# Splitting two feature groups of the last MLP by pairs of tiles

## Chip, cores, metric

The kernel runs on one core of one Trainium2 chip, alone. The metric is the device time of one execution in microseconds (us); the number given for a kernel is the median of its runs.

## What is computed

One transformer block for 1024 tokens of width 1024: a mixer of two sparse attentions, cross-attention to a memory of 256 tokens, and an MLP, each added to the residual stream.

```
x = x + mixer(rms_norm(x, norm1_g), ...)
x = x + memory_xattn(rms_norm(x, norm2_g), mem, ...)        # 4 heads of 128, w_xq, w_xk, w_xv, w_xo
x = x + square(relu(rms_norm(x, norm3_g) @ w_ff_in)) @ w_ff_out   # 1024 -> 4096 -> 1024
```

All values are float32. Where precision asks for it, the kernel splits an operand into a high part in a short format (hi, `xh`, `whi`, `hh`) and the remainder (lo, `xl`, `wlo`, `hl`), and multiplies hi by hi, hi by lo and lo by hi, so that one product is three matmuls.

## The kernel before

The 1024 tokens are eight tiles of 128. After the projections, the work runs in two streams that are written side by side: the sparse attention of tile after tile, and beside it whatever is ready of the rest. The rest goes through `between` (L902: output projection of the mixer, then memory attention) and `mlp` (L1002). `between` takes two tiles at a time, `mlp` four. When the sparse attention is through, what remains is `between` of tiles 4 and 5 (in pool `dn`) beside `between` of tiles 6 and 7 (in pool `d2`), and then `mlp` of tiles 4 to 7, alone.

The instruction order on each engine is not the program's: the tile framework schedules it from a timeline of its own (`schedule_with_timeline_sim`), and each engine, and SP's queue of DMA issues, then goes through its list in order.

In `mlp`, 4096 features are eight groups (`f4`) of 512. For each group the first layer makes four PSUM tiles of 128 features by all tokens of the call (512 columns, stationary `w_ff_in`, moving `xh`, `xl`; 24 matmuls each). ScalarE takes the relu and the square (L1034, L1035), GpSimd the split into `hh` and `hl` (L1037, L1038, ring `h` of eight buffers). The second layer then makes, for each half `c` of the output columns and each tile, one PSUM tile (12 matmuls, stationary `hh`, `hl`, moving `w_ff_out`), which VectorE adds to the residual stream `x2` (L899). TensorE writes these PSUM tiles in turn to two buffers.

Weights come by `load_w` (L251): a DMA into ring `wraw`, the cast `whi` on ScalarE (L244) and the remainder `wlo` on GpSimd or VectorE (L249, two of three on GpSimd in this last part, `PLAN_TAIL`). A group needs sixteen such loads of 256 KB. Rings of pool `d2` for it: `wraw` 3, `whi` 6, `wlo` 6. `between` loads its own weights whole, without a split, into the rings `whi` and `wlo` by turns (`load_whole`, L261).

Before the MLP stands a norm (`norm_T2`, L290): a square with a sum on ScalarE (L293), a power on GpSimd, and for each half of a tile a product with the gain on VectorE (L297), four transposes on TensorE into PSUM (L274), then hi on ScalarE and lo on VectorE (L235, L236). The gain (`gain2`, L340) lies in two buffers of ring `h`.

At the end of memory attention, for two heads at a time (`memory_item`, L939): scores, exponentials (L966), transposes of the probabilities (L972), values, and a store of the result to memory (L986), which is read back (L992), transposed and multiplied by `w_xo`. After `between` of tiles 4 and 5 the residual stream goes out to memory (L1000) and is read back by `mlp` (L1007); that of tiles 6 and 7 stays in its buffers.

Of the kernel before, what the change touches and what calls it, by code (L numbers as in the profile page):

```python
# [22 lines left out]
P = 128  # L23
# [13 lines left out]
    "p1": {"x4": 5, "st": 2, "relu": 4, "wraw": 4, "whi": 6, "wlo": 6, "c8": 4, "c4": 2, "kraw": 5, "pc": 2},  # L37
    "p2": {"x4": 3, "st": 1, "relu": 2, "whi": 4, "wlo": 4, "c8": 3, "c4": 1, "kraw": 4, "pc": 2},
    "dn": {"b4": 4, "h": 8, "relu": 2, "wraw": 2, "whi": 4, "wlo": 4},
    "d2": {"b4": 4, "h": 8, "relu": 2, "wraw": 3, "whi": 6, "wlo": 6},  # L40
}
PSUMS = {"p1": {"D": 4, "M": 3, "C": 1}, "main": {"S": 2, "PT": 2, "PV": 1, "D": 2, "M": 1}}
TAGS = {"p1": ("D", "M", "C"), "p2": ("D", "M", "D"), "dn": ("D", "M"), "d2": ("S", "PT")}
PLAN_HEAD = ("ag", "av")
PLAN_MAIN = ("ag",)
PLAN_TAIL = ("ag", "av", "ag")
# [37 lines left out]
def drain(gen):  # L84
    for _ in gen:
        pass
# [19 lines left out]
def merge(a, b):  # L106
    drain(beside(*a, *b))
# [59 lines left out]
def build(nc, tc, I, C, out):  # L167
# [13 lines left out]
    def pst(tag, shape):  # L181
        return psum["pool"].tile(shape, F32, tag=tag, name="ps" + tag, bufs=psum["n"][tag],
                                 padded_shape=[P, 512 // int(np.prod(shape[2:]))] + list(shape[2:]))

    def ring(pool, tag, shape, dt=F32):
        n = RINGS[pool.name if isinstance(pool.name, str) else "dn"][tag]
        return pool.tile(shape, dt, tag=tag, name=tag, bufs=n)
# [63 lines left out]
    def load_w(pool, shape, *srcs):  # L251
        raw = ring(pool, "wraw", shape)
        for dst, src in srcs:
            nc.sync.dma_start(dst(raw), src)
        hi, lo = ring(pool, "whi", shape, F32R), ring(pool, "wlo", shape, F32R)
        split_w(raw, hi, lo)
        return hi, lo
# [32 lines left out]
    def norm_T2(pool, x_t, gb, xs):  # L290

        ss = small(pool, "nss", 1)
        s.activation(xs[0], x_t.rearrange("p (k c) -> p k c", c=P), AF.Square, accum_out=ss)  # L293
        r = rsqrt_of(pool, ss, DM, 1, "n")
        for c in range(0, DM, 512):
            xn = ring(pool, "relu", [P, 512])
            v.scalar_tensor_tensor(xn, x_t[:, c:c + 512], r[:, 0:1], gb[c // 512], op0=ALU.mult, op1=ALU.mult)  # L297
            to_T(pool, xn, [x[:, c // P:c // P + 4] for x in xs], 4)
# [29 lines left out]
    def xT(pool, nt, whole=False):  # L328

        parts = [pool.tile([P, DM // P, nt * P], F32 if whole else F32R, tag="x" + n, name="x" + n)  # L330
                 for n in ("h" if whole else "hl")]
        return (parts, [lambda t, k, x=x: x[:, k, t * P:(t + 1) * P] for x in parts],
                lambda t: [x[:, :, t * P:(t + 1) * P] for x in parts])
# [668 lines left out]
    def mlp(pool, t0, nt, x2s):  # L1002
# [13 lines left out]
        for f4 in range(8):  # L1016
# [24 lines left out]
            for c in range(2):  # L1041
# [4 lines left out]
                for t in range(nt):  # L1046
# [11 lines left out]
                                          x2[t][:, c * 512:(c + 1) * 512])  # L1058
                    yield 2.6

    def pe_stack():
        pe = p1.tile([P, 2, 32], F32R, tag="pe", name="pe")
        pe2 = ring(p1, "relu", [P, 2, 2, 64])
        for j in range(2):
            nc.sync.dma_start(pe2[0:32, :, j, :], W["nsa_cmp_pe"].rearrange("k l d -> l k d"))
        pp = pst("M", [P, 2, 32])
        for kv in range(2):
            te.transpose(pp[:, kv, :], pe2[0:32, kv, :, :].rearrange("p a d -> p (a d)"), ident[0:32, 0:32])
        s.activation(pe, pp, AF.Copy)
        v.tensor_tensor(pe[64:128], pp[64:128], pe[64:128], op=ALU.subtract)  # L1070
        return pe
# [49 lines left out]
    d2_pool = tc.tile_pool(name="d2", bufs=1, side="right", reuse_waits="tile")  # L1121
    plan["w"] = PLAN_TAIL
    d2 = d2_pool.__enter__()
    x2s = {}
    rest = (w for w in rest if not isinstance(w, tuple))
    merge((rest, REST), (between(d2, 6, 2, x2s, True), 45.0))
    dn_pool.__exit__(None, None, None)
    drain(mlp(d2, 4, 4, x2s))
    d2_pool.__exit__(None, None, None)
    ctx.close()  # L1130

# [20 lines left out]
```

## Time and profile before

| | |
|---|---|
| median of 3 runs | 1833.72 us (1833.55 to 1837.51) |
| profiled execution | 1835.75 us, its span 1833.9 us |
| mean clock granted to TensorE | 0.97 |
| busy share PE, PEld, DVE, ACT, POOL | 94%, 80%, 51%, 59%, 49% |

PE is TensorE's matmuls and PEld its weight loads, DVE is VectorE, ACT ScalarE, POOL GpSimd, SP the engine that issues most DMAs. In a timeline a row is start, length, engine, line, instruction, output and inputs by the program's names without buffer numbers, shape, count, and in brackets the idle time before it and what ended that. Matmuls overlap, so the distance of two starts, not the length, is what one costs. In a row of windows, the length is followed by the busy time (and number of instructions) of each engine, the clock granted to TensorE (1.00 is full), the share of DMA engines in use and the GB/s moved.

### The profile page before, as it was taken

The page shows a single profiled execution, that of the slowest core. Times are in us where ns is not written, and L with a number is a line of the kernel's source. Part 1 is how long each engine was busy: PE and PEld are TensorE (multiplying, and loading weights), DVE is VectorE, ACT ScalarE, POOL GpSimd, SP SyncE. Part 2 cuts the span into 40 slices and gives each one's busy share as a digit, 9 for nine tenths or more (in the row PEclk, how much of TensorE's full clock was granted, in tenths as well). Part 3 has the DMA queues.
Part 4 walks back from the last instruction along what each step waited for, and adds up shares of the span by engine and source line. Part 5 has one row for each costly group of instructions (what it writes and reads, how often), then busy time and mean ns, then how long its engine had stood idle before and what let it go on. Part 6 is the DMA issues. An engine that isn't in the chain of part 4 may idle for free. (4 is left out here: it accounts for less than half of the span.)

```text
span 1833.9 us, 28049 instructions
## 1 busy us (share of the span) xinstructions
PE 1726.9 (94%) x9262; PEld 1474.2 (80%) x9262; DVE 936.1 (51%) x2353; ACT 1074.6 (59%) x2687; POOL 895.0 (49%) x1034
## 2 busy tenths in 40 slices
PE   5996999889989998999999999999999799999999
PEld 5995988777878787778887788888988578787787
DVE  4553766575684678466664656646523422222222
ACT  4444658889588669955797457994412323333332
POOL 2364657446262244677676576662111144454443
PEclk9997998999999999999999999999989799999999
DMA  8224512256335320222112112125394222222232
GB/s 203 70 87 160 103 34 79 78 193 180 122 112 162 120 81 24 73 81 71 64 63 91 54 65 75 60 79 185 99 288 131 71 69 92 92 93 93 94 99 98
DMA packets 180081, 187.50 MB, mean 102 GB/s; under 512 B 34656, under 2 KB 149088, under 8 KB 179936
## 3 DMA queue, kind: packets, MB, share of 16 engines
q1 hardware_dynamic: 172000, 175.23, 30.8%
q0 software_dynamic: 7936, 10.49, 2.2%
q8 instruction: 73, 1.20, 0.3%
q14 instruction: 72, 0.59, 0.1%
HBM read 164.69 MB, written 20.97 MB: 101 GB/s over the span
## 5 line engine op out<-in xcount | busy, mean ns | idle before, releaser
L249 POOL TENSOR_TENSOR wlo<-wraw,whi 128x512 fp32r<-128x512 f32 (+1 forms) x230 | 308.5, 1347 | 278.7 <-ACT whi L244 247.6
L244 ACT ACTIVATE whi<-wraw 128x512 fp32r<-128x512 f32 (+2 forms) x289 | 181.1, 628 | 247.4 <-PE psS L218 147.1
L218 PE MATMUL psD<-whi,xh 128*128 128x256 f32 (+1 forms) x704 | 193.8, 359 | 3.6 <-ACT whi L244 2.9
L218 PE MATMUL psD<-wlo,xh 128*128 128x256 f32 (+1 forms) x704 | 194.8, 357 | 0.8 <-DMA wlo<-in_w_in_dram 0.8
L236 DVE TENSOR_TENSOR pl<-psPT,ph 128x512 fp32r<-128x512 f32 (+1 forms) x232 | 142.2, 621 | 78.2 <-ACT ph L235 75.4
L218 PE MATMUL psD<-whi,h 128*128 128x512 f32 x512 | 174.3, 404 | 1.8 <-POOL h L1037 1.0
L688 ACT ACTIVATE S<-S,mn 128x128 f32<-128x128 f32 (+7 forms) x192 | 142.7, 744 | 41.5 <-DVE mn L686 40.3
L218 PE MATMUL psS<-whi,h 128*128 128x512 f32 x512 | 162.1, 392 | 5.1 <-DVE b L899 5.1
L693 POOL TENSOR_SCALAR S<-S,sums,gi 128x640 f32<-128x640 f32 (+7 forms) x128 | 107.7, 850 | 106.7 <-DVE sums L691 99.0
L235 ACT ACTIVATE ph<-psPT 128x512 fp32r<-128x512 f32 (+1 forms) x232 | 122.8, 540 | 60.9 <-PE psPT L703 54.5
L249 DVE TENSOR_TENSOR wlo<-wraw,whi 128x512 fp32r<-128x512 f32 (+1 forms) x59 | 64.3, 1090 | 166.9 <-ACT whi L244 166.8
L218 PEld LDWEIGHTS psD<-whi,xh 128*128 128x128 f32 x704 | 134.0, 198 | 14.3 <-ACT whi L244 3.3
L218 PEld LDWEIGHTS psD<-wlo,xh 128*128 128x128 f32 x704 | 134.8, 197 | 12.5 <-DMA wlo<-in_w_in_dram 1.2
L703 PE MATMUL psPT<-c_ident,S 128*128 128x128 f32 x816 | 132.3, 279 | 8.3 <-DVE ql L236 4.2
L899 DVE TENSOR_TENSOR b<-psS,b 128x512 f32<-128x512 f32 (+1 forms) x80 | 50.0, 635 | 152.6 <-PE psS L218 152.6
L218 PEld LDWEIGHTS psS<-whi,h 128*128 128x128 f32 x512 | 96.1, 188 | 29.3 <-DVE b L899 9.3
L218 PE MATMUL psS<-K,qh 128*128 128x384 f32 (+3 forms) x288 | 113.5, 397 | 5.6 <-DVE mn L686 2.8
L218 PEld LDWEIGHTS psD<-whi,h 128*128 128x128 f32 x512 | 95.6, 190 | 23.7 <-DVE b L899 1.5
L703 PEld LDWEIGHTS psPT<-c_ident,S 128*128 128x128 f32 x816 | 98.1, 143 | 18.9 <-POOL S L693 5.6
L218 PE MATMUL psD<-wlo,h 128*128 128x512 f32 x256 | 102.5, 404 | 1.3 <-POOL wlo L249 1.3
L218 PE MATMUL psD<-xh,wlo 128*128 128x512 f32 x256 | 101.5, 398 | 0.0
L899 DVE TENSOR_TENSOR b<-psD,b 128x512 f32<-128x512 f32 (+1 forms) x112 | 63.2, 572 | 74.5 <-PE psD L218 73.0
(299 smaller groups left out, 4647.4 us busy)
## 6 DMA issues: line engine op xcount, KB each, us to landing
wraw<-in_w_ff_in_dram SPq DMA_DIRECT2D x128, 256.0 KB, 2.7
wraw<-in_w_ff_out_dram SPq DMA_DIRECT2D x128, 256.0 KB, 2.6
whi<-in_w_out_dram SPq DMA_DIRECT2D x32, 256.0 KB, 5.0
wlo<-in_w_out_dram SPq DMA_DIRECT2D x32, 256.0 KB, 4.6
wraw<-in_w_in_dram SPq DMA_DIRECT2D x24, 256.0 KB, 3.1
q<-st SPq DMA_DIRECT2D x12, 512.0 KB, 2.6
qin<-q SPq DMA_DIRECT2D x44, 128.0 KB, 2.3
x<-in_x_dram SPq DMA_DIRECT2D x8, 512.0 KB, 5.2
```

The lines of the kernel that those rows point to most:

```text
L218: te.matmul(o, a, b, start=start, stop=stop)
L235: s.activation(hi, src, AF.Copy)
L236: v.tensor_tensor(lo, src, hi, op=ALU.subtract)
L244: s.activation(hi, raw, AF.Copy)
L249: (v if l == "v" else g).tensor_tensor(lo, raw, hi, op=ALU.subtract)
L688: s.activation(S, S, AF.Exp, bias=low, scale=-1.0, accum_out=sums[:, hh:hh + 1])
L693: g.tensor_scalar(Ss[hh], Ss[hh], sums[:, hh:hh + 1], 1.0 if gate is None else gate[:, hh:hh + 1], op0=ALU.mult, op1=ALU.mult)
L703: te.transpose(p2[:, j, hh, :], S[:, (c + j) * P:(c + j + 1) * P], ident)
L899: v.tensor_tensor(dst, pt, dst, op=ALU.add)
```

## The change

`mlp` for tiles 4 to 7 gives way to a new function, `mlp_tail`, in a pool `d3` of its own with larger rings for split weights (`wraw` 4, `whi` 8, `wlo` 8). Of the eight feature groups the first two are done by pairs of tiles: for tiles 4 and 5 first, then groups 2 to 7 for all four tiles, then groups 0 and 1 for tiles 6 and 7. So these two groups' weights are loaded and split twice, and their first-layer matmuls stream 256 columns. The norm of tiles 4 and 5 comes ahead of the pair's groups, that of tiles 6 and 7 after them in the program. The pool lies where `dn` lay, beside `d2`, in which memory attention of tiles 6 and 7 still runs; `d2` loses `wraw`, and its rings for whole weights go from 6 and 6 buffers to 5 and 5. The PSUM tags are `D` and `M`, before `S` and `PT`; `M` has one buffer, `PT` two. `between` of tiles 6 and 7 no longer keeps the residual stream on chip: it goes out to memory and is read back. The outputs of tiles 4 and 5 leave as one write each when groups 2 to 7 are done.

In the order that the scheduler gives the changed program, the first pair group stands among the last instructions of memory attention of tiles 6 and 7, the second one behind them, and the transposes of the norm of tiles 6 and 7 behind that.

```diff
-    "d2": {"b4": 4, "h": 8, "relu": 2, "wraw": 3, "whi": 6, "wlo": 6},
+    "d2": {"b4": 4, "h": 8, "relu": 2, "whi": 5, "wlo": 5},
+    "d3": {"b4": 4, "h": 8, "relu": 2, "wraw": 4, "whi": 8, "wlo": 8},
...
-TAGS = {"p1": ("D", "M", "C"), "p2": ("D", "M", "D"), "dn": ("D", "M"), "d2": ("S", "PT")}
+TAGS = {"p1": ("D", "M", "C"), "p2": ("D", "M", "D"), "dn": ("D", "M"), "d2": ("S", "PT"), "d3": ("D", "M")}
...
+    def mlp_tail(pool, t0, G):
+
+        x2 = {}
+        (xh, xl), _, xt_of = xT(pool, 4)
+
+        def start(t, gb3):
+            x2[t] = ring(pool, "b4", [P, DM])
+            nc.sync.dma_start(x2[t], x2_dr[t0 + t])
+            norm_T2(pool, x2[t], gb3, xt_of(t))
+
+        def group(f4, ts, last):
+            cols = slice(ts[0] * P, (ts[-1] + 1) * P)
+            n = len(ts) * P
+            hs = []
+            for f2 in range(2):
+                gr = []
+                for k0 in range(0, 8, KG):
+                    c0 = (f4 * 4 + f2 * 2) * P
+                    hi, lo = load_w(pool, [P, KG, 256], (lambda r: r, W["w_ff_in"][k0 * P:(k0 + KG) * P, c0:c0 + 256]
+                                                         .rearrange("(k p) n -> p k n", p=P)))
+                    gr += [(hi[:, k, :], lo[:, k, :]) for k in range(KG)]
+                for f in range(2):
+                    pt = pst(TAGS[pool.name][0], [P, n])
+                    fs = slice(f * P, (f + 1) * P)
+                    for k in range(8):
+                        wh, wl = gr[k]
+                        mm(pt, wh[:, fs], xh[:, k, cols], k == 0, False)
+                        mm(pt, wl[:, fs], xh[:, k, cols], False, False)
+                        mm(pt, wh[:, fs], xl[:, k, cols], False, k == 7)
+                    r = ring(pool, "relu", [P, n])
+                    s.activation(r, pt, AF.Relu)
+                    s.activation(r, r, AF.Square)
+                    hh, hl = ring(pool, "h", [P, n], F32R), ring(pool, "h", [P, n], F32R)
+                    g.tensor_scalar(hh, r, 1.0, 1.0, op0=ALU.mult, op1=ALU.mult)
+                    g.tensor_tensor(hl, r, hh, op=ALU.subtract)
+                    hs.append((hh, hl))
+            for c in range(2):
+                gr = []
+                for k in range(4):
+                    r0 = (f4 * 4 + k) * P
+                    gr.append(load_w(pool, [P, 512], (lambda r: r, W["w_ff_out"][r0:r0 + P, c * 512:(c + 1) * 512])))
+                for t in ts:
...
+                    dst = x2[t][:, c * 512:(c + 1) * 512]
+                    v.tensor_tensor(dst, pt, dst, op=ALU.add)
+                    if last:
+                        nc.sync.dma_start(out[0, (t0 + t) * P:(t0 + t + 1) * P, c * 512:(c + 1) * 512], dst)
+
+        for ts in ((0, 1), (2, 3)):
+            gb3 = gain2(pool, W["norm3_g"])
+            for t in ts:
+                start(t, gb3)
+            if ts[0] == 0:
+                for f4 in range(G):
+                    group(f4, ts, False)
+        for f4 in range(G, 8):
+            group(f4, (0, 1, 2, 3), False)
+        for t in (0, 1):
+            nc.sync.dma_start(out[0, (t0 + t) * P:(t0 + t + 1) * P, :], x2[t])
+        for f4 in range(G):
+            group(f4, (2, 3), f4 == G - 1)
...
-    x2s = {}
     rest = (w for w in rest if not isinstance(w, tuple))
-    merge((rest, REST), (between(d2, 6, 2, x2s, True), 45.0))
+    merge((rest, REST), (between(d2, 6, 2, {}, False), 45.0))
     dn_pool.__exit__(None, None, None)
-    drain(mlp(d2, 4, 4, x2s))
+    with tc.tile_pool(name="d3", bufs=1, reuse_waits="tile") as d3:
+        mlp_tail(d3, 4, 2)
```

More of the change, by code (lines that the diff above doesn't have):

```diff
@@ L1059, in mlp @@
                     yield 2.6
+    def mlp_tail(pool, t0, G):
[37 more added lines that the diff above has]
+                for t in ts:
+                    pt = pst(TAGS[pool.name][0], [P, 512])
+                    us = slice((t - ts[0]) * P, (t - ts[0] + 1) * P)
+                    for f in range(4):
+                        hh, hl = hs[f]
+                        wh, wl = gr[f]
+                        mm(pt, hh[:, us], wh, f == 0, False)
+                        mm(pt, hh[:, us], wl, False, False)
+                        mm(pt, hl[:, us], wh, False, f == 3)
+                    dst = x2[t][:, c * 512:(c + 1) * 512]
[15 more added lines that the diff above has]
+            group(f4, (2, 3), f4 == G - 1)
```

## The prediction

> **What bounds the kernel now.** I read the page first, then the chain of waits, then the windows of the last 400 us, and last the timelines of single engines there.
>
> ```profile
> span 1833.9 us, 28049 instructions
> PE 1726.9 (94%) x9262; PEld 1474.2 (80%) x9262; DVE 936.1 (51%) x2353; ACT 1074.6 (59%) x2687; POOL 895.0 (49%) x1034
> ```
> ```profile
> 1469.14 28.00 PE psS L218 x119
> ...
> 1633.26 44.15 PE psS L218 x191
> ...
> 1677.43 0.70 DVE b L899
> ...
> 1813.53 16.63 PE psS L218 x72
> ...
> 1830.18 0.69 DVE b L899
> ```
>
> The second fence is the chain (start, length, what). From 1469 to 1830 us it is the matmuls of the last MLP and almost nothing else: a feature group is 192 matmuls of 512 columns, 44.15 us and one residual add of 0.70 on which TensorE waits (its PSUM buffer), 44.9 in all. After the last matmul come 3.7 us (1833.9 less 1830.2). So the MLP itself leaves nothing to gain; what can be gained lies just before it:
>
> ```profile
> 1425.00:1430.00 5.00, 4.32 (x18) 3.50 (x19) 1.80 (x5) 2.67 (x8) 0.00 (x0) 0.57 0.30 105
> 1430.00:1435.00 5.00, 3.24 (x16) 3.05 (x15) 0.85 (x2) 0.00 (x0) 0.00 (x0) 0.50 0.21 43
> 1435.00:1440.00 5.00, 3.06 (x9) 2.34 (x10) 0.00 (x0) 0.60 (x1) 0.00 (x0) 0.50 0.33 117
> 1455.00:1460.00 5.00, 1.99 (x12) 1.11 (x10) 2.18 (x7) 4.38 (x9) 2.48 (x4) 0.98 0.28 95
> 1460.00:1465.00 5.00, 3.09 (x13) 2.15 (x12) 4.99 (x9) 2.67 (x5) 0.95 (x2) 0.50 0.00 0
> ```
> ```profile
> 1420.52 0.38 PE L274 MATMUL psPT<-c_ident,relu 128*128 128x128 f32 x2
> 1428.29 4.96 PE L218 MATMUL psS<-h 128*128 128x128 f32 x22 [0.42 <-ACT h L235]
> 1436.25 1.09 PE L274 MATMUL psPT<-c_ident,relu 128*128 128x128 f32 x4 [3.01 <-DMA relu<-xo]
> 1453.81 1.03 PE L218 MATMUL psS<-whi,xh 128*128 128x256 f32 x4
> 1454.68 1.03 PE L218 MATMUL psS<-wlo,xh 128*128 128x256 f32 x4
> 1458.68 1.34 PE L274 MATMUL psPT<-c_ident,relu 128*128 128x128 f32 x8 [2.98 <-DVE relu L297]
> 1468.79 0.78 PE L218 MATMUL psS<-xh,whi 128*128 128x512 f32 x1
> ```
>
> Windows (length, busy PE, PEld, DVE, ACT, POOL, then clock, DMA, GB/s) and TensorE's timeline show one stretch, 1420.5 to 1468.8, 48.3 us: the end of memory attention of tiles 6 and 7, to 1455.5, then 13.3 us in which only the norm of four tiles runs. TensorE has gaps there and is granted half its clock for most of it. All attention work of it, at full clock, is some 22 us (its output projection alone is eight blocks of 1.73: the two rows at 1453.81 and 1454.68, 0.87 apart, are half a block).
>
> **The change: what stays equal.** The MLP keeps its multiplications, but in two feature groups each first-layer matmul now streams 256 columns and is issued twice as often.
>
> ```profile
> 44.31 0.28 PE L218 MATMUL psD<-whi,xl 128*128 128x256 f32 x1
> 44.43 0.29 PE L218 MATMUL psD<-whi,xh 128*128 128x256 f32 x1
> ...
> 1471.29 0.39 PE L218 MATMUL psS<-xh,whi 128*128 128x512 f32 x1
> 1471.52 0.40 PE L218 MATMUL psS<-xh,wlo 128*128 128x512 f32 x1
> ```
>
> At full clock 256 columns start 0.115 to 0.12 us apart and 512 columns 0.23. A pair's group is 96 x 0.115 + 48 x 0.23 = 22.1 us, half of 44.2. TensorE is not charged for the split. The price must come from waits.
>
> **First pair group, beside attention of tiles 6 and 7.** Up to that attention's second half the engines' orders differ little. Then three queues change.
>
> ```profile
> 1411.76 0.34 SPq L1000 DMA_DIRECT2D x<-b  x1
> 1414.48 0.32 SPq L1007 DMA_DIRECT2D b<-x  x1
> 1415.13 0.32 SPq L1000 DMA_DIRECT2D x<-b  x1
> 1419.84 0.32 SPq L1007 DMA_DIRECT2D b<-x  x1
> 1433.74 0.42 SPq L986 DMA_DIRECT2D xo<-relu  x1
> 1436.57 0.32 SPq L992 DMA_DIRECT2D relu<-xo  x1
> ```
> ```profile
> wraw<-in_w_ff_in_dram SPq DMA_DIRECT2D x5, 256.0 KB, 2.7
> b<-x SPq DMA_DIRECT2D x2, 512.0 KB, 3.8
> h<-in_norm_g_dram SPq DMA_DIRECT2D x2, 256.0 KB, 3.4
> ```
>
> The rings of attention's own weights shrink from twelve buffers to ten. I cost that at nothing, since ten are still two column blocks of four ahead; if that cover fails, it is one landing, 2.7 us.
>
> SP: in the changed order the second half of the norm gain goes out before both reloads of x2, and it waits for the store of tile 5 (its buffer lies on that tile's). That store needed from 1415.1 to 1419.8. So tile 4 is reloaded at about 1420.1 (before 1414.5) and lands about 1423; the first MLP weight, behind it, lands about 1424.
>
> ```profile
> 1424.29 0.56 ACT L966 ACTIVATE relu<-psS,xnb,xsc 128x256 f32<-128x256 f32 x1 [1.38 <-DVE xnb L963]
> 1444.52 0.63 ACT L244 ACTIVATE whi<-wraw 128x512 fp32r<-128x512 f32 x1 [1.22 <-PE psS L218]
> 1455.79 1.06 ACT L293 ACTIVATE xh<-b 128x1024 fp32r<-128x1024 f32 x1 [0.28 <-PE psS L218]
> 1460.60 0.68 DVE L236 TENSOR_TENSOR xl<-psPT,xh 128x512 fp32r<-128x512 f32 x1
> 1461.20 0.74 DVE L297 SCALAR_TENSOR_TENSOR relu<-b,nr,h 128x512 f32<-128x512 f32 x1
> ```
>
> ScalarE: ahead of the softmax's first exponentials (1424.3 before) now stand two squares of the norm (1.06 each), five weight casts (0.63) and two copies of the norm. The fifth cast is what costs: four raw buffers, so its load goes out only when VectorE is through with the first weight. Square of tile 5 ends about 1426, first cast 1426.7, its remainder (0.68) about 1428.1, load 2.7, cast to 1431.5, copy, and the exponentials start at about 1432 and 1434 (a sixth cast between them). That is 8 us late. Behind them wait both transposes of the probabilities, the value matmuls and the store.
>
> The Trainium skill, "TensorE: Matmul & The Clock Gate", section "Architectural detail", says that ScalarE and VectorE are strict FIFOs and only TensorE pulls weight loads ahead. By it the 8 us stand; were the queue free to pass a waiting cast, this part would end some 5 us sooner, near 1833 for the whole. No run here shows a pass, and the sum goes by the order of the queue.
>
> TensorE then has 19 pair matmuls at half clock (0.23) ahead of the last ten value matmuls, 4 us more: these end about 1445, before about 1433. The store and reload of the result need 2.8 us from issue to issue (1433.74 to 1436.57) and 2.7 to land: 1450.5. From there I count work without gaps: attention's projection (eight blocks of 1.73, 13.8), the pair's second layer (48 x 0.23 = 11.1) and the last 24 first-layer matmuls (2.8), 27.7 in all, and 2 more for transposes and for the matmuls ahead of the reload. The first pair group and attention end at about 1480, where before the full MLP had begun at 1468.8: 22 us of work taken in for 11.
>
> **Second pair group.** It stands alone, after attention, and its weights arrive as they are split.
>
> ```profile
> 1633.30:1678.20 44.90, 44.35 (x193) 35.91 (x193) 11.39 (x14) 14.79 (x24) 22.23 (x19) 1.00 0.30 94
> 1633.30:1678.20 44.90, 25.08 (x64) 12.03 (x64) 6.06 (x5) 14.77 (x11) 1.00 0.30 94
> 1633.30:1678.20 44.90, 22.26 (x97) 17.86 (x97) 0.00 (x0) 0.00 (x0) 7.64 (x8) 1.00 0.30 94
> ```
>
> These are one full group, its wlo instructions alone and its h alone. GpSimd's 14.77 us for eleven weight remainders stays per group whether two tiles use it or four; its 7.64 for h halves. So 18.6 us must fit into 22.1, and with them the sixteen casts of 0.63 that a pair's group repeats (10.1 on ScalarE, and half as much again for the squares) and sixteen more loads; over two groups 32 each, all beside TensorE unless a queue holds them. It fits, but not in order: a group's last h stands behind two or three remainders of 1.34. On TensorE I count 0.7 for the residual add that holds PSUM and 1.0 for that h, 23.8 a group, and 1 more here because two reloads of x2 stand between the weights: 24.9, to 1505.
>
> **Norm of tiles 6 and 7.** The pair group that should hide it cannot: the gain is loaded into h buffers of the group just running, last read 9 matmuls (2.1 us) before its end, and then takes 3.4 to land and 0.74 for the first product. Its four half-tiles go through one PSUM buffer: a copy (as long as a cast, 0.63) and a remainder (0.68) must follow each set of transposes (1.09) before the next may start, 2.4 us, and one product of 0.74 that VectorE puts between raises the mean to 2.65. Three rounds come before the wide matmuls: -2.1 + 3.4 + 0.74 + 3 x 2.65 = 10, and about 2 for half clock after it: 12, to 1517. Before it was 13.3.
>
> **Sum, on the profiled execution.** 1517 + 6 full groups x 44.9 + 2 pair groups (tiles 6 and 7) x 23.8 + 3.7 = 1837.7, against a span of 1833.9: 3.8 slower. The execution's own time is 1835.75, its overhead 1.9; the median of the runs is 1833.72. I put the difference on the median: 1837.5.
>
> The outputs of tiles 4 and 5 now leave before the last two groups, as two writes on SP's queue that wait for residual adds; behind them stand the second layer's weights of the next group. They are costed at nothing, because the first layer's eight weights, 11 us of TensorE's work, are already past them; if not, the price is a landing of 2.7.
>
> Bounds: end of the first part 1475 (TensorE's own work, 44, after 1420.5, with some 10 us in which nothing is loaded yet) to 1484; second group 22.8 to 27; norm 10 to 14; last groups 22.8 to 26 each. All low: 1826; all high: 1850. I took values near the queue walk, not the middle.
>
> **Rivals.** *Faster (0.21):* the place is the exponentials behind the fifth cast. If store and loads land a microsecond or two sooner each and TensorE has sustained work by 1431, exponentials come 5.5 us sooner and half-clock work shrinks by 3: 1837.5 - 8.5 = 1829. It decides where the exponentials start before 1427. For it: DMA is only 0.3 busy at 1425; against it: no clock row rises before TensorE has worked some 7 us (half clock 1430 to 1440 with 3 of 5 us busy). The same page of the Trainium skill, section "What's actually happening", gives about 3.4 us of sustained work for the rise; by that the time would be nearer to this rival.
> *Slower, starved pairs (0.24):* each group's sixteen weights need one per 1.39 us; a raw buffer's turn is 2.7 + 0.63 + 1.34 = 4.7 for four, 1.17. If a load takes over 3.6 us, or casts wait in line for as long, the turn passes 4 x 1.39 = 5.6 and decides: three lone groups that lose 4 each make 1837.5 + 12 = 1850. For it: other loads took 3.4 and 3.8; against it: DMA at 0.30 in the full group.
> *Forecast (0.55):* the three parts nearly cancel, 1831 to 1844.
>
> **How the numbers follow.** 0.2% is 3.7 us, about what a measurement of this kernel can tell from no change. Faster: the first rival and 0.01 of the forecast, 0.22. Within: 0.25, from the forecast. Slower: the rest of it, 0.29, and the starved pairs, 0.53. Range 1828 to 1850: the rivals' values with both tails left out.
>
> **What would show it.** Right: exponentials of tiles 6 and 7's second heads near 1432; attention's last projection matmul near 1477; wide matmuls only from 1515 on; a gap of 8 to 12 us before them, ended by a gain's DMA. Wrong: no such gap, pair groups over 26 us, full groups other than 44.9, or a changed time before 1400.

## The result and the profile after

The changed kernel takes 1851.26 us (median of 1846.43, 1851.02, 1851.51 and 1852.38) against 1835.28 us before (the three runs above and a fourth, 1836.84): a ratio of 1.0081, 95% interval 1.0059 to 1.0104. It is slower by 15 to 16 us. Run again later beside new runs of the kernel before it took 1850.81 against 1837.87, ratio 1.0072 (1.0053 to 1.0091). The forecast was 1837.5 and the range ended at 1850: the side was right, the size was not.

The profiled execution of the changed kernel is its quickest, 1846.43 us with a span of 1844.3; the rerun's profiled execution took 1851.29 with a span of 1849.2. Both are used below, as "the first profile" and "the rerun". The page of the first profile:

```profile
span 1844.3 us, 28688 instructions
PE 1727.9 (94%) x9454; PEld 1482.4 (80%) x9454; DVE 947.9 (51%) x2364; ACT 1094.0 (59%) x2735; POOL 931.9 (51%) x1071
```

TensorE is busy for 1.0 us more than before, in a span 10.4 us longer. So the price is idle time, as the prediction had it; halving the columns of 96 matmuls a group costs next to nothing (0.3 us a group, below). The chain of waits shows where it lies:

```profile
1471.41 1.74 PE psS L219 x8
...
1477.92 3.52 DMA b<-x
...
1484.60 3.42 POOL wlo L250 x2
...
1504.02 3.85 DMA h<-in_norm_g_dram
...
1516.04 2.07 PE psD L219 x4
...
1591.44 44.43 PE psD L219 x191
1635.87 0.02 issue
1635.90 0.70 DVE b L1113
...
1796.78 1.75 POOL wlo L250
...
1802.41 2.96 DMA wraw<-in_w_ff_in_dram
...
1806.16 1.02 POOL wlo L250
```

Before, nothing but matmuls and a residual add a group (two in some) stood here from 1469 on. Now the chain leaves TensorE in three places: in the second pair group (GpSimd's remainders, behind the reload of x2), at the norm of tiles 6 and 7 (the gain's DMA), and in the first of the two last pair groups (a remainder, then a weight that has not landed, then a remainder again). The same in windows (length, then busy PE, PEld, DVE, ACT, POOL, then clock, DMA share, GB/s): second pair group, wait for the norm, a full group, the two last groups:

```profile
1476.20:1505.80 29.60, 25.67 (x145) 20.97 (x143) 8.27 (x12) 15.55 (x30) 20.54 (x22) 0.94 0.52 170
1505.80:1516.00 10.20, 3.20 (x13) 1.92 (x12) 5.89 (x8) 2.51 (x5) 2.02 (x2) 0.64 0.42 140
1591.40:1636.60 45.20, 44.65 (x192) 36.08 (x192) 11.61 (x14) 14.59 (x24) 22.58 (x19) 1.00 0.28 94
1789.10:1816.10 27.00, 24.29 (x144) 20.85 (x144) 8.53 (x9) 12.03 (x25) 18.19 (x19) 0.94 0.48 156
1816.10:1840.10 24.00, 23.44 (x147) 20.29 (x145) 7.10 (x8) 9.04 (x18) 15.06 (x16) 1.00 0.34 121
```

GpSimd has 20.5 us of work in the second pair group, for which TensorE needs 22.1; the prediction had counted 18.6. Of the two last groups only the first is slow: counted from first matmul to first matmul it takes 27.4 us (28.9 in the rerun) and the last one 23.6 (23.9), near the 23.8 of the forecast. Behind the last one no other group's weights have to be loaded and split. TensorE's timeline says what it waited for there and in the norm:

```profile
1494.89 0.50 PE L219 MATMUL psD<-whi,h 128*128 128x512 f32 x1 [0.87 <-POOL h L1095]
1497.28 0.73 PE L219 MATMUL psD<-whi,h 128*128 128x512 f32 x2 [1.19 <-POOL h L1096]
1508.42 0.89 PE L275 MATMUL psM<-c_ident,relu 128*128 128x128 f32 x4 [2.50 <-DVE relu L298]
1511.64 1.09 PE L275 MATMUL psM<-c_ident,relu 128*128 128x128 f32 x4 [2.32 <-DVE xl L237]
1514.27 1.09 PE L275 MATMUL psM<-c_ident,relu 128*128 128x128 f32 x4 [1.54 <-DVE xl L237]
```

The first two rows wait for the hidden values' split on GpSimd, the last two for the one PSUM buffer to be read out.

SP's queue has waits of its own in the second pair group (in all, times, longest, in us):

```profile
SPq L255 <- POOL wlo L250: 8.1, 8, 2.4
SPq L1069 <- DMA x<-b: 3.9, 1, 3.9
```

In the first row the load of a weight waits for a remainder on GpSimd; until that is made, its raw buffer is not free. In the second the reload of tile 7 waits for its store to land, and the second layer's weights stand behind it.

The part by part account, in span time (first matmul of a part to first matmul of the next; the gap before the wide matmuls counts from the last matmul's end):

| part | forecast | first profile | rerun |
|---|---|---|---|
| end of attention and first pair group | 1480 | 1476.2 | 1479.0 |
| second pair group | 24.9 | 29.6 | 28.5 |
| to the first wide matmul | 10 | 10.2 | 10.3 |
| six full groups, with the slow clock at their start | 2 + 269.4 | 273.1 | 274.5 |
| two last pair groups | 47.6 | 51.0 | 52.8 |
| to the end | 3.7 | 4.2 | 4.2 |
| span | 1837.7 | 1844.3 | 1849.2 |

### The profile page after: what moved, and what is told of

Same layout as the page of the kernel before. It is cut to its first block, busy times and chain, and to the rows that moved or that the text cites. A ratio compares the mean times of both kernels' runs of the same rounds, so it can differ in the third digit from the quotient of the medians.

```text
span 1844.3 us, 28688 instructions
## 1 busy us (share of the span) xinstructions
PE 1727.9 (94%) x9454; PEld 1482.4 (80%) x9454; DVE 947.9 (51%) x2364; ACT 1094.0 (59%) x2735; POOL 931.9 (51%) x1071
## 4 chain that ended last, share of the span: by engine, by line
PE 70%; DVE 9%; ACT 6%; DMA 6%; POOL 5%; issue 4%; SPq 1%; POOLq 0%; DVEq 0%; ACTq 0%
PE psD L219 48%; PE psS L219 9%; PE psPV L219 5%; PE psPT L704 4%; ACT dmask L645 2%; POOL wlo L250 2%; PE psM L275 1%; DMA wraw<-in_w_ff_in_dram 1%; DVE S L687 1%; DVE pl L237 1%; PE psPT L591 1%; DMA wraw<-in_w_ff_out_dram 1%; ACT tkt L647 1%; ACT tks L646 1%; DVE relu L298 1%
## 5 line engine op out<-in xcount | busy, mean ns | idle before, releaser
L219 PE MATMUL psD<-whi,h 128*128 128x512 f32 x1024 | 344.0, 405 | 11.6 <-DVE b L1113 5.0
L245 ACT ACTIVATE whi<-wraw 128x512 fp32r<-128x512 f32 x321 | 200.8, 628 | 227.7 <-PE psD L219 145.3
L219 PEld LDWEIGHTS psD<-whi,h 128*128 128x128 f32 x1024 | 193.3, 190 | 62.7 <-DVE b L1113 8.9
L219 PE MATMUL psD<-xh,wlo 128*128 128x512 f32 (+1 forms) x576 | 212.9, 370 | 0.0
L219 PE MATMUL psD<-xh,whi 128*128 128x512 f32 (+1 forms) x576 | 211.2, 371 | 1.3 <-ACT xh L236 0.7
L219 PE MATMUL psD<-xl,whi 128*128 128x512 f32 (+1 forms) x576 | 212.3, 370 | 0.0
L219 PE MATMUL psD<-wlo,h 128*128 128x512 f32 x512 | 205.3, 403 | 1.3 <-POOL wlo L250 1.3
L219 PEld LDWEIGHTS psD<-xh,whi 128*128 128x128 f32 x576 | 108.5, 189 | 19.4 <-ACT xh L236 1.1
L219 PEld LDWEIGHTS psD<-xh,wlo 128*128 128x128 f32 x576 | 108.7, 189 | 17.5 <-POOL wlo L250 0.3
L219 PEld LDWEIGHTS psD<-xl,whi 128*128 128x128 f32 x576 | 108.6, 189 | 16.0
```

The costliest lines, as they stand in the source:

```text
L219: te.matmul(o, a, b, start=start, stop=stop)
L245: s.activation(hi, raw, AF.Copy)
```

## The experiments

Each kernel was timed beside the kernel before on the same chip; a ratio is against that. "Changed kernel" is the one of the diff. Four theories were put up: A, the turn of the raw weight buffers starves the pair groups that stand alone (the prediction's rival); B, the loss is the uncovered norm; C, the rebuilding costs and not the pairs; D, GpSimd's order of work starves the lone groups.

**again**: no edit.

> The changed kernel once more, unchanged. Its profiled execution had a span of 1844.3 us, its other runs 1848.9 to 1850.3. If the 5 us come from one place (a queue that falls into another order in some executions), a second profile of about 1849 shows where: both theories below put it into the two-tile groups that stand alone (1476 to 1506 and 1789 to 1840 in the first profile). If the profile is again near 1844 and the runs near 1850, the place stays open.

1850.81 us. The second profile is one of the usual length, and no single place holds its 5 us: the reload of x2 is issued 1.2 us later than in the first (1415.75 against 1414.53), the first pair group ends 2.8 later, the norm is 1.7 behind, the two last groups take 1.8 more. So the executions differ by a microsecond or two here and there, and the kernel before varies as much (1832.83 to 1843.74 in that session).

**one_pair_group** and **no_pair_group**: `mlp_tail(d3, 4, 2)` becomes `mlp_tail(d3, 4, 1)`, and `mlp_tail(d3, 4, 0)`. Without pair groups the four writes of tiles 6 and 7's output, which stand in the last one, fall away too.

> Only feature group 0 is done by pairs of tiles; seven groups take all four tiles. Theory A (the two-tile groups that stand alone are starved of split weights): the second pair group, 29.6 us instead of half a full group's 22.6, and the second of the two last ones go, the norm of tiles 6 and 7 follows the first pair group, still uncovered (its residual stream is reloaded at 1476.7 and 1481.5): wide matmuls from about 1489, 2.6 us of half clock, 7 x 45.1, one pair group of 25, 4: a span of 1834 to 1838, 6 to 10 us less than the changed kernel. Theory B (the loss is the uncovered norm and the lone groups cost only their matmuls): the uncovered norm stays, so 1841 to 1845. Theory C (the restructuring, not the pairs, costs): no difference to the changed kernel.

> No feature group is done by pairs; new pool, larger rings, residual stream of tiles 6 and 7 out and back, one PSUM buffer for the norm's transposes all stay. Theory A: attention ends near 1455 as before the change, the store and reload of tiles 6 and 7 (4 + 4 us) and their norm follow: wide matmuls from 1470 to 1476, then 8 x 45.15 and 4: 1835 to 1841. Theory C: as slow as the changed kernel, 1844 or more.

One group: 1841.96 us, ratio 1.0022 (1.0008 to 1.0035); its profile's span of 1840.3 lies 2 us above theory A's range and just below B's. None: 1850.56, ratio 1.0069 (1.0051 to 1.0087), which is some 10 us above what theory A had and as slow as with two. So the loss is not simply "the pairs": without them, the rebuilding alone costs 12 to 13 us. Its chain of waits:

```profile
1442.10 3.44 DMA relu<-xo
...
1452.70 14.13 PE psS L219 x56
...
1467.31 2.81 DMA x<-b
...
1470.13 4.22 DMA b<-x
...
1482.39 2.07 PE psD L219 x4
```

Attention's result comes back from memory at 1445.5, its projection runs to 1466.8 where it ended about 1455.5 before, and then tiles 6 and 7 go out to memory and back (7 us) and through their norm (8 us) with nothing beside them: wide matmuls from 1482.4, before from 1468.8. The first pair group earns most of this back (8.6 us from none to one) by filling attention's gaps; the second, placed alone, gave away what the first had earned (8.9 us from one to two).

**own_gain**: the gain of the last norm loaded once, into two buffers of its own.

```diff
+        gb3 = gain2(pool, W["norm3_g"], "gb")
         for ts in ((0, 1), (2, 3)):
-            gb3 = gain2(pool, W["norm3_g"])
```

> The gain of the last norm is loaded once into two buffers of its own, instead of twice into buffers of the ring of split hidden values; two pair groups stay. The order then has the norm's transposes of tiles 6 and 7 among the second pair group's second layer. Theory A and B: the gap of 10 us before the wide matmuls goes, all but about 2 (the transposes still share one PSUM buffer): 1834 to 1837 against 1844.3. If the gain is not what the norm waits for (the reload of the residual stream or the PSUM buffer is): 1841 to 1844.

1839.96 us, ratio 1.0011 (0.9996 to 1.0025): 11 to 13 us off the changed kernel. Second pair group and norm together take 35.2 us (1476.2 to 1511.4) instead of 39.8, so the gain's wait was worth 4.6 (3.6 against the rerun's 38.8) and not the whole gap; the transposes still wait for each other and for VectorE inside the group. The rest was not expected: from there to the last groups 269.5 us instead of 273.1. Each full group took 44.66 us instead of 45.20, though nothing in it was edited (hidden_ring_last, below). The two last groups took 53.3 us, no less than in the changed kernel.

**more_raw** and **h_on_vector**: larger rings; the hidden values' split of pair groups on VectorE.

```diff
-    "d3": {"b4": 4, "h": 8, "relu": 2, "wraw": 4, "whi": 8, "wlo": 8},
+    "d3": {"b4": 4, "h": 8, "relu": 2, "wraw": 8, "whi": 10, "wlo": 10},
```

```diff
-                    g.tensor_scalar(hh, r, 1.0, 1.0, op0=ALU.mult, op1=ALU.mult)
-                    g.tensor_tensor(hl, r, hh, op=ALU.subtract)
+                    (g.tensor_scalar(hh, r, 1.0, 1.0, ...) if n == 512 else v.tensor_copy(hh, r))
+                    (g if n == 512 else v).tensor_tensor(hl, r, hh, op=ALU.subtract)
```

> Rings of the last MLP only: raw weight buffers 8 instead of 4, split weights 10 and 10 instead of 8 and 8. Theory A (a raw buffer's turn starves the lone pair groups): the second pair group falls from 29.6 us to 24 to 25 and the last two from 51 to 46 to 47, 8 to 10 us off: a ratio to the kernel before of about 1.002 against 1.008. Theory D (GpSimd, which goes in order through remainders and hidden-value splits, starves them): 0 to 3 us off, ratio 1.006 to 1.008.

> In the pair groups VectorE makes both halves of the hidden values' split, GpSimd only the weight remainders; rings as in the changed kernel. Theory D: the second pair group falls to 24 to 25.5 us and the last two to 47 to 48, 6 to 8 us off, ratio 1.003 to 1.005. Theory A: the casts still wait for loads, 0 to 3 us off, ratio 1.006 to 1.008.

more_raw: 1845.89 us, ratio 1.006 (1.0043 to 1.0078). h_on_vector: 1843.05, ratio 1.0035 (1.002 to 1.0049). By the times D explains more than A. Windows of the second pair group and of the two last, first more_raw, then h_on_vector:

```profile
1478.70:1505.70 27.00, 24.10 (x145) 19.68 (x143) 9.32 (x12) 14.31 (x29) 21.21 (x22) 1.00 0.59 189
1789.30:1837.70 48.40, 46.12 (x289) 40.16 (x287) 15.10 (x17) 20.05 (x40) 32.20 (x33) 1.00 0.36 114
```
```profile
1480.00:1507.30 27.30, 23.80 (x145) 19.87 (x143) 14.41 (x20) 15.27 (x30) 14.67 (x14) 1.00 0.59 186
1791.60:1838.90 47.30, 45.51 (x289) 40.31 (x287) 23.63 (x33) 21.10 (x42) 23.68 (x18) 1.00 0.47 150
```

Either edit takes 3 to 5 us out of the last two groups (51.0 and 52.8 without), nearly all of it from the first of them, and 1 to 3 out of the second pair group, so theory D alone is not the whole of it either. They are not exclusive: a late weight and a full GpSimd hold TensorE by turns, as the chain of the changed kernel had it (remainder, DMA, remainder). more_raw also made the rings of split weights larger, so it does not show by itself that it was the raw ring; SP's waits for remainders, above, speak for that.

**keep_67**: the residual stream of tiles 6 and 7 stays on chip, as before the change (`between(d2, 6, 2, x2s, True)`, and `start` takes the kept buffer).

> The changed kernel, but the residual stream of tiles 6 and 7 stays in its buffers, as before the change: no store, no reload, and the second pair group's weights no longer stand behind that reload on SP. If these two reloads hold that group (the prediction gave them 1 us): its 28.2 to 29.6 us fall by 2 to 4, ratio 1.005 to 1.0065. If GpSimd's order alone does: under 1 us, ratio 1.007 to 1.008. The norm of tiles 6 and 7 still waits for the gain, so its gap stays near 10 us.

1848.99 us, ratio 1.0056 (1.0036 to 1.0077); 3 to 5 us off by the ratios, whose intervals overlap. The window is clearer: with the store and the reload gone from SP's queue the second pair group takes 25.4 us, 3 to 4 less than in the changed kernel, while the gap before the wide matmuls stays at 10.3.

```profile
1478.40:1503.80 25.40, 23.60 (x145) 19.82 (x143) 8.73 (x10) 12.63 (x25) 19.48 (x20) 1.00 0.56 174
```

**own_gain_more_raw**, **own_gain_more_raw_h_vector** and **all_three_keep_67**: these edits together.

> Own buffers for the gain and the larger rings together. Theory A: both savings add, since they lie in different stretches: own_gain had a ratio of 1.0011, 8 to 10 us off it: 1.829 to 1.832 ms, ratio 0.995 to 0.997, faster than before the change. Theory D: ratio 0.999 to 1.001.

> The same with the hidden values' split of pair groups on VectorE. If raw buffers and GpSimd's order each hold TensorE in turn, this is the first kernel whose lone pair groups come near their 22.1 us of matmuls: 1.824 to 1.829 ms, ratio 0.993 to 0.995. If the rings alone do it, the same as the kernel without this edit; if neither, 0.999 to 1.001.

> Own gain, larger rings and hidden values' split on VectorE (ratio 0.9958), and the residual stream of tiles 6 and 7 kept. Here the norm no longer waits for the gain, but its square stands behind the reload (1479 to 1485 in that profile), and the second pair group took 29.2 us with the norm's transposes in it. If the reload holds both: 2 to 5 us off, ratio 0.993 to 0.995. If not: 0.995 to 0.9965.

1832.55 us, ratio 0.9978 (0.9965 to 0.9991); 1826.89, ratio 0.9958 (0.9944 to 0.9972); 1827.77, ratio 0.9945 (0.9925 to 0.9965). All three beat the kernel before, the last two by 8 to 10 us (between them the measurement does not tell), so the plan of the change works once its waits are gone. Some 2.4 us of each gain are not the plan's: the full groups take 44.67 us here and 45.07 in the kernel before, by closer matmuls (hidden_ring_last, below) and fewer waits for a residual add. So most of the first one's 4 us may be that. The two last groups of own_gain_more_raw_h_vector:

```profile
1779.30:1825.50 46.20, 45.06 (x289) 40.30 (x287) 23.95 (x33) 20.05 (x40) 22.27 (x17) 1.00 0.37 120
```

46.2 us for matmuls that need 44.2; the forecast had 47.6 for these two. With both edits the waits that it had undercharged are gone.

**first_casts_gpsimd** and **squares_off_scalar**: what delays attention. First the casts of the first pair group go from ScalarE to GpSimd and all its remainders to VectorE (`plan["w"] = ("gv",)` for that group), then the squares of the norm of tiles 4 and 5, for these two alone, go to GpSimd and their sums to VectorE.

```diff
-        s.activation(xs[0], x_t.rearrange("p (k c) -> p k c", c=P), AF.Square, accum_out=ss)
+        xk = x_t.rearrange("p (k c) -> p k c", c=P)
+        g.tensor_tensor(xs[0], xk, xk, op=ALU.mult)
+        v.tensor_reduce(ss, xs[0], axis=AX.XY, op=ALU.add)
```

> The changed kernel, but the sixteen weights of feature group 0 for tiles 4 and 5 are cast by GpSimd, their remainders made by VectorE; no cast stands ahead of the second heads' exponentials on ScalarE any more. If ScalarE's order is what delays attention (the prediction's step): exponentials at about 1427 and 1429 instead of 1429 to 1430 and 1433 to 1434, attention's last projection matmul 3 to 5 us earlier (1468 to 1471), ratio 1.005 to 1.006 against 1.0072 to 1.0081. If the delay is elsewhere (a reload, the half clock), the last projection matmul stays at 1472 to 1475 and the ratio too; if GpSimd's casts starve the first pair group, it ends later than 1479 and the ratio rises.

> The changed kernel, but the two squares of the norm of tiles 4 and 5 are made by GpSimd and summed by VectorE; on ScalarE attention's square and its first copy of the second heads now come ahead of anything that needs the reloaded residual stream. If ScalarE's wait for that reload (4.6 us idle ahead of the square, in the profile of the changed kernel run again) is what delays attention: that copy at about 1420 instead of 1422.8, exponentials 2 to 4 us earlier (1426 to 1428 and 1428 to 1431 instead of 1430.1 and 1433.7), attention's last projection matmul at 1469 to 1472, ratio 1.005 to 1.0065. If VectorE's order (norm products, remainders, the new sums, ahead of the softmax's maxima) is: exponentials no earlier than 1429 and the ratio 1.007 to 1.008.

Without the casts the exponentials start at 1430.68 and 1434.75, no earlier than in the rerun (1430.11 and 1433.7); 1848.52 us, ratio 1.0063 (1.0048 to 1.0077). In both kernels ScalarE's idle time just ahead of the exponentials is ended by VectorE, which had more remainders to make without the casts; so this run shows that the casts were not the last thing waited for, and not that they cost nothing. Without the squares, ScalarE's timeline, the rerun's two rows first (a reload that has not landed at the head of the queue, and attention's copy behind it), then that of squares_off_scalar:

```profile
1421.47 1.06 ACT L294 ACTIVATE xh<-b 128x1024 fp32r<-128x1024 f32 x1 [4.62 <-DMA b<-x]
1422.79 0.37 ACT L236 ACTIVATE h<-psPT 128x256 fp32r<-128x256 f32 x1
```
```profile
1420.20 0.38 ACT L236 ACTIVATE h<-psPT 128x256 fp32r<-128x256 f32 x1
1427.24 0.55 ACT L972 ACTIVATE relu<-psS,xnb,xsc 128x256 f32<-128x256 f32 x1
```

The copy comes 2.6 us earlier, the first exponential 2.9, and attention's last four projection matmuls start at 1467.9 instead of 1474.9. So the reload at the head of ScalarE's queue is what delays attention's copy, and with it the exponentials. Yet the kernel took 1855.33 us, ratio 1.0093 (1.0071 to 1.0115): the first pair group now ends at 1486.5 instead of 1479.0. Two windows say where TensorE lost it, those of the rerun first, then those of squares_off_scalar, and a row of its ScalarE:

```profile
1440.00:1450.00 10.00, 10.00 (x81) 10.00 (x80) 1.81 (x3) 4.82 (x10) 3.88 (x5) 0.91 0.42 135
1470.00:1480.00 10.00, 10.00 (x50) 8.48 (x49) 2.83 (x5) 1.74 (x4) 2.58 (x2) 1.00 0.73 241
```
```profile
1440.00:1450.00 10.00, 8.83 (x50) 7.93 (x49) 1.97 (x4) 3.02 (x5) 1.27 (x1) 0.71 0.22 65
1470.00:1480.00 10.00, 6.86 (x32) 5.33 (x31) 4.25 (x5) 5.84 (x11) 8.35 (x8) 0.99 0.90 290
```
```profile
1473.65 1.06 ACT L299 ACTIVATE xh<-b 128x1024 fp32r<-128x1024 f32 x1 [1.80 <-DMA b<-x]
```

While attention's result goes out and back, fewer matmuls of the pair are at hand, and the clock stays low (0.71); and after attention the square of tile 6 takes the place that tile 4's had: it waits for its reload on ScalarE, the pair group's last casts behind it. The pair group had been covering attention's delay. What the better order would be was not found.

**hidden_ring_last**: the same instructions, on every engine and in SP's queue in the same order, at other addresses; the rings `b4`, `relu`, `wraw`, `whi`, `wlo` are laid out before `h`.

```diff
+        for tag in ("b4", "relu", "wraw", "whi", "wlo"):
+            for _ in range(RINGS[pool.name][tag]):
+                ring(pool, tag, ...)
```

> The changed kernel with one thing altered: the ring of split hidden values lies at the end of the pool (111776 bytes into a partition instead of 50336), the rings of weights where own_gain has them within 5 KB. Every engine's order is the same. If the place of the buffers is why a full group took 44.66 us in own_gain and 45.20 here (second-layer matmuls 0.2275 against 0.2334 us apart): 44.66 us a group, about 4 us off in all, ratio 1.005 to 1.006. If it is something else (the phase of the ring, the gain's buffers): 45.20, ratio 1.007 to 1.008.

1844.48 us, ratio 1.0038 (1.0024 to 1.0052), 6 to 8 us off. The chain gives a full group's matmuls 43.62 us, against 44.43 in the changed kernel:

```profile
1591.52 43.62 PE psD L219 x191
```

**all_three_keep_67_place** puts these addresses into the best kernel (with rings of 8 for split weights, where it had 10).

> all_three_keep_67 with the buffers of xh, xl, split weights and split hidden values at the addresses that they have in hidden_ring_last (split weights in rings of 8, raw weights 8, at the end of the pool). If the place of these buffers sets the distance of the matmuls: full groups 44.39 us instead of 44.66, about 2 us off in all: ratio 0.992 to 0.995. If the raw and other buffers' places count too, groups anywhere from 44.4 to 45.2.

Its groups take 44.4 us too (43.60 to 43.81 in the chain, after 43.90 to 43.92), so the place carries over. Its ratio, 0.9971 (0.9959 to 0.9982), overlaps that of all_three_keep_67, and the gain of some 2 us is not to be seen in the times.

**all_three_keep_67_one_group**: one pair group instead of two.

> all_three_keep_67 with one feature group by pairs instead of two. If the second pair group pays because it covers the norm of tiles 6 and 7: this norm follows attention uncovered (8 to 10 us), against some 5 us that the second pair group takes beyond its half group and 1 to 2 at the end: 2 to 4 us slower than with two, ratio 0.996 to 0.998. If one group is enough: 0.992 to 0.9945.

1831.33 us, ratio 0.9985 (0.9976 to 0.9993). The norm of tiles 6 and 7 is uncovered again (wide matmuls 9.2 us after the first pair group). With the waits gone the second pair group pays; with them it cost 9 us (one_pair_group against the changed kernel).

**all_three_two_psum**, **all_four_casts_gpsimd** and **all_three_keep_67_squares** were to improve on the best kernels and did not. The first is own_gain_more_raw_h_vector with one edit more, the second is the first with the casts on GpSimd, the third is all_three_keep_67 with the squares off ScalarE.

> Own gain, larger rings, hidden values' split on VectorE, and the norm's transposes in the two PSUM buffers that attention's transposes use, instead of the single one. If the single buffer is what the norm of tiles 6 and 7 still waits for inside the second pair group (1.07 to 2.01 us in front of transposes, behind the remainder on VectorE): 2 to 4 us off the kernel without this edit, whose ratio was 0.9958: 0.9935 to 0.995. If not, 0.995 to 0.9965.

> The same with feature group 0's casts for tiles 4 and 5 on GpSimd. If ScalarE's order delays attention, the 3 to 5 us of first_casts_gpsimd add to the others: ratio 0.991 to 0.993, about 1820 us. If GpSimd starves the first pair group, slower than the kernel without this edit.

> The same with the squares of tiles 4 and 5 off ScalarE. If both attention's delay and the reload cost what the two single runs show, this is the fastest: 0.991 to 0.9935. If attention's delay is VectorE's order, the same as the kernel without this edit.

1838.50 us, ratio 1.0008 (0.9995 to 1.0021); 1838.35, 1.0011 (0.9999 to 1.0022); 1832.94, 0.9974 (0.9961 to 0.9986). In the first the norm's transposes share their PSUM buffers with attention's and the scheduler puts them behind it: attention's last four projection matmuls start at 1462.2, earliest of all, but the first pair group ends at 1490.1 (1491.9 in the second run). These two say the same as squares_off_scalar: what counts is when attention and the first pair group are both done, and attention going first ended later. The third does not show it: its first pair group ends at 1483.5 against 1482.3 in all_three_keep_67, within what two profiles differ by.

## Why the prediction was right or wrong, point by point

**TensorE is not charged: right.** In the first profile the 96 matmuls of 256 columns from 1789.14 to 1800.34 start 0.118 us apart, where half of a 512-column distance in the same kernel is 0.1145: 0.3 us a group. TensorE's busy time grew by 1.0 us.

**End of the first part, 1480: right (1476.2, 1479.0), partly by luck, and for another reason than given.** Attention's last projection matmul starts at 1472.8, in the rerun at 1475.6 (forecast near 1477). The exponentials were forecast for 1432 and 1434 and started at 1429.1 and 1432.8, in the rerun at 1430.1 and 1433.7. But the step blamed the fifth cast, and with every cast gone from ScalarE (first_casts_gpsimd) the exponentials came no earlier. The wait stands earlier in the queue: ScalarE idles for 5.22 us (4.62 in the rerun) ahead of the norm's square, because the reload of tile 4 takes 5.8 us to land (5.5 in the rerun), where the prediction put it at 3. It had also placed that reload at 1420.1, behind the store of tile 5; the two stores went out earlier than before and it was issued at 1414.5. Two errors of some 3 and 5.6 us had opposite signs; that they nearly cancel is the luck. The rows are SP's issue of the reloads and ScalarE's square in the first profile:

```profile
1414.53 0.85 SPq L1069 DMA_DIRECT2D b<-x  x2
```
```profile
1420.50 1.06 ACT L294 ACTIVATE xh<-b 128x1024 fp32r<-128x1024 f32 x1 [5.22 <-DMA b<-x]
1432.75 0.56 ACT L967 ACTIVATE relu<-psS,xnb,xsc 128x256 f32<-128x256 f32 x1 [1.89 <-DVE xnb L964]
```

The last row, the second pair of exponentials, waits for VectorE, which the step did not walk: norm products and remainders stand there ahead of the softmax's bias, and the bias itself is slow. It is one product of two columns; VectorE's timeline before, and the chain of the first profile, for both pairs of exponentials:

```profile
1424.02 0.15 DVE L963 TENSOR_TENSOR xnb<-xnb,xsc 128x2 f32<-128x2 f32 x1
```
```profile
1427.89 1.22 DVE xnb L964
...
1431.52 1.14 DVE xnb L964
```

0.15 us became more than 1.1, while GpSimd was making remainders; before, it stood idle there. In squares_off_scalar the product took 0.15 us at 1426.15, with no remainder beside it, and 1.22 at 1430.51, beside one. No run tests this cause alone.

What the prediction took from the Trainium skill, "TensorE: Matmul & The Clock Gate", section "Architectural detail", that ScalarE is a strict FIFO, agrees with the trace: attention's copy, which ran at 1420.20 where no square stood ahead of it (squares_off_scalar), waited behind the square until 1422.79 in the rerun. From the same page of the Trainium skill, section "What's actually happening", the prediction drew that a rise of the clock after 3.4 us would bring the time nearer to the faster rival. The first half holds here better than my 7 us of work:

```profile
1433.40:1437.40 4.00, 3.99 (x21) 4.00 (x22) 2.74 (x5) 3.05 (x8) 1.34 (x1) 0.55 0.38 114
1437.40:1441.00 3.60, 3.60 (x34) 3.60 (x33) 1.11 (x2) 1.20 (x2) 0.00 (x0) 1.00 0.43 149
```

Full clock came after some 4 us without a gap. How much of the 1 to 4 us by which the first part ended early this was worth is not shown; the lone groups lost more.

**Second pair group, 24.9: wrong, 28.5 to 29.6. Two last groups, 47.6: wrong, 51.0 to 52.8.** This is the step that failed, by 8 to 9 us, and with it the choice between forecast and rival. (The 24.9 is 23.8 and 1, which make 24.8.) The prediction saw that GpSimd's 18.6 us must fit into 22.1 "but not in order", and then charged 1.7 a group for the wait on the hidden values' split and on the residual add. That was enough for the last group (23.6 and 23.9 against 23.8), which has no weights of a next one beside it (the likely reason; no run tests it alone), and not for the two that have: 28.5 to 29.6 and 27.4 to 28.9. It computed the raw buffers' turn as 1.17 us a weight against 1.39 and let that pass. Each is under its limit alone, at 84%; together they are over it, since a remainder late on GpSimd keeps a raw buffer (8.1 us of SP's waits), which makes the next weight late, which makes a remainder late. With both relieved (own_gain_more_raw_h_vector) the two last groups take 46.2. The starved-pairs rival had the place and most of the size (+12 for three groups; measured +8 to +9), but named the raw ring as the one cause; more_raw (rings) and h_on_vector (GpSimd's queue) each take a part away. Of the second group's excess, 3 to 4 us came from the store and reload of tiles 6 and 7 ahead of its weights on SP (keep_67), which the prediction had put at 1: it had not counted that the reload of tile 7 waits 3.9 us on the queue for its own store.

**Norm of tiles 6 and 7: right.** A gap of 10.2 us (forecast 8 to 12), ended by a gain's DMA (3.85 in the chain), three rounds through one PSUM buffer, wide matmuls from 1516.0 (forecast from 1515 on). That they start so near to it is luck, since the second pair group began 3.8 us early and took 4.7 too long. own_gain took 4.6 us out of second pair group and norm together, and the rounds remain.

**Full groups, 44.9: short by 0.3 each.** 45.20 here, over six groups 1.8 us. In the kernel before, the quoted chain rows at 1633.26 and 1813.53 are four groups apart, 45.07 each: 44.9 was one group's row, and one group in four there waits for a second residual add. That is not what the 0.3 is made of here: each group waits for one add, as in the row that was read, but its matmuls take 44.43 us instead of 44.15. They start further apart (last section). What is left of the rerun's 3.1 us is the slow clock at the start, 3.3 us instead of 2.

**Outputs of tiles 4 and 5, and smaller weight rings of attention, at nothing: no wait on them shows in the chain.** No run tested either alone. Up to 1400 the time hardly changed: the first profile stands 0.6 us ahead of the old one at that point.

**The rest.** These errors on the rerun, -1.0 + 3.6 + 0.3 + 3.1 + 5.2 + 0.5, make the 11.5 us between 1837.7 and 1849.2 (rounding apart). The range's upper end, 1850, was the sum of all high bounds; the high bound of 26 us for a last group, twice, was met in the rerun (52.8), and the second group's 27 was passed.

## What to carry to other kernels

Where two resources are each at some 85% of what a stage allows and feed each other through a ring, do not count them as hidden one by one: give each slack (deeper ring, other engine) before the stage is shortened. Half as much TensorE work per weight halves the cover of everything that is per weight: loads, casts, remainders, and any reload that stands in their queue. And where one piece of work fills the gaps of another, letting the one go first can make the end of both later, as squares_off_scalar did.

## What the runs showed of the hardware that was not expected

The place of buffers in a partition changes the distance of matmuls. With the same instruction order, a full group took 45.20 us with `h` at byte 50336 (`whi` from 95584, `wlo` from 111968) and 44.39 with `h` at 111776 (`whi` from 79008, `wlo` from 95392); the second layer's matmuls start 0.2334 and 0.2272 us apart on average, the first layer's 0.2290 and 0.2267. In own_gain (`h` at 116064, `whi` from 83296) they are 0.2275 and 0.2291, in the kernel before (`h` at 185760) 0.2270 and 0.2319. more_raw moved `whi` and `wlo` by 8 and 12 KB, left `h` where it was, and kept the 45.20; that speaks for the place of `h`, but no run moves `h` alone. Which rule is behind it stays open; over six groups it is 5 us, about what the smaller edits here gained or lost.

Executions of one order differ before the changed part begins: in three profiles of the same order on every engine, SP issued the reload of tile 4 at 1414.53 (the first profile), 1415.75 (the rerun) and 1411.89 (hidden_ring_last, in whose row both reloads stand). In all_three_keep_67, with another order, it was 1418.49. So a difference of two profiles' ends of some 4 to 7 us says little here; lengths of parts and medians do.

```profile
1411.89 1.21 SPq L1072 DMA_DIRECT2D b<-x  x2
```
